# A streaming encoder layer on one core: earlier weights for the second unit, later gates in the last

## The chip, the cores and the metric

The kernel runs on one core of one Trainium2 chip. The metric is the time of one execution on the device in microseconds (us), the median of several runs. TensorE (PE in the profile) multiplies, VectorE (DVE), ScalarE (ACT) and GpSimd (POOL) do the elementwise work, and nearly all transfers are issued from the queue of SyncE (SP).

## The reference

One layer over 2048 prompt frames of one stream and 16 new frames of each of eight running streams (128 rows, with caches of 512 past positions). Rows are normed and modulated by a conditioning vector, then projected by `w_in` to ten groups of columns. A differential attention (four heads, two softmaxes each) and a stick-breaking attention (eight heads, a running product over the keys instead of a softmax) take three groups each; two groups are SiLU gates `za`, `zb`, and two are the merge gates `ga`, `gb`:

```python
qa, ka, va, za, qb, kb, vb, zb, ga, gb = jnp.split(h @ w_in, idx, axis=-1)
...
    ya = (oa.reshape(b, s, WIDTH_A) * jax.nn.silu(za)) @ w_branch_a
    yb = (ob.reshape(b, s, WIDTH_B) * jax.nn.silu(zb)) @ w_branch_b
    return (jax.nn.sigmoid(ga) * ya + jax.nn.sigmoid(gb) * yb) @ w_out
...
        xp = xp + gate * merge_branches(...)
...
    y_prompt = rms_norm(xp, final_g)
```

Everything is float32 outside. New keys and values are outputs too.

## The kernel before

Rows are worked in 17 tiles of 128: tiles 0 to 15 are the prompt, tile 16 (`NT`) is the sample. To keep float32 accuracy, each operand of a large product is split into a float16 high and low part, scaled by a power of two that comes from a norm of the matrix, and three products (high-high, high-low, low-high) are summed. So every weight block is loaded, squared and summed on ScalarE (`sum_squares`, L295), its scale is worked out (`scales`, on VectorE, with a product with ones on TensorE), and then it is split (`split`, L315 or L317 for the high part, L320 for the low).

The first stage norms and modulates the input and writes it transposed and split to `hT_d`. The middle stage, where most of the time goes, has eight units: unit u has head pair u // 2 and kind u % 2 (0 is the differential attention, 1 the stick-breaking). A step is a unit and a tile, 136 in all, the sample tile first in each unit. A step of a prompt tile makes the scores of its queries against all earlier keys (`scores`, products L697, L698, mask product L701), the softmax or the stick-breaking weights (for kind 1: sigmoids L131, scan L671, product on GpSimd L677, cast L605, rest L608), a transposing DMA (L615), and later the products with the values (L754 to L759). The weighted values go to `o_d`.

Beside attention, two lists of pieces are dealt out by hand:
- `line` holds the projections (24 products per tile, L461). In units of odd number each tile's projection is followed by 12 gate pieces of two products each (L537), which make 512 columns of the merge gates; ScalarE copies them out of the PSUM bank `ps_t` (L540) and they go to `g_d`. The line runs about `LEAD` = 5 steps ahead of attention. The input tile is fetched (`fetch_h`, L438) into one of three buffers `hs`, and is held there until its gate pieces have run.
- `side` pieces: `prepare_unit` loads, squares and splits the next unit's weights, in units with gates 22 pieces; `norms` has two lists, the squares of late weights and cached values (49 pieces, `spare`, loads L920) and the splitting of the cached keys (`cached`). `norm_at` and `keys_at` say in which steps they are dealt out.

When the line is empty, `early_work` prepares the output stage: the remaining branch weights and the first two tiles. The output stage (`branches` L1471, `output` L1508) runs over the tiles 0 to 14, then the sample tile, then tile 15, with the sample's attention as a second lane beside its first tiles. The conditioning gate of the sample tile has nine rows in `gate_d`, which are spread over its 128 rows by a product with `sel`.

The order of an engine's instructions is laid down when the kernel is built: a planner goes through the instructions in program order with a cost model and lets a later instruction pass one that is not yet ready. An instruction marked with `kept` passes no earlier one of its engine.

Of the kernel before, what the change touches and what calls it, by code (L numbers as in the profile page):

```python
# [17 lines left out]
F32 = mybir.dt.float32  # L18
# [3 lines left out]
AF = mybir.ActivationFunctionType  # L22
ALU = mybir.AluOpType
# [3 lines left out]
P = 128  # L27
# [31 lines left out]
H_AT = 2  # L59
Q_BUFS = 6  # L60
TR_AFTER = 5
LEAD = 5.0
TILE_TIME = 0.6
SAMPLE_TIME = 0.3
# [57 lines left out]
def layer_kernel(ctx: ExitStack, tc: tile.TileContext, a: dict):  # L122
# [14 lines left out]
    def kept(x):  # L137
        tc.keep_in_program_order(x)
        return x
# [68 lines left out]
    def bank(tag, dt=F32):  # L208
        return ps.tile([P, 512 if dt == F32 else 1024], dt, tag=tag, name=f"ps_{tag}", bufs=BANKS[tag])
# [222 lines left out]
    silu_z = {}  # L432
    at_hand, ahead, fetched = {}, {}, []

    def fetch_h(u, t):
        ahead[u, t] = hs[len(fetched) % 3].bitcast(F16).rearrange("p (f k n) -> p f k n", f=2, n=P)
        fetched.append(t)
        load(out=ahead[u, t], in_=hT_d[t // 4][:, t % 4, :, :, :])  # L438

    def project(U, t):  # L440
# [89 lines left out]
        def gate_piece(n):  # L530

            if n == 0:
                box["g"] = bank("t")
            for j in range(per * n, per * n + per):
                hi, wi = ((0, 0), (0, 1), (1, 0))[j % 3]
                k = j // 3
                T.matmul(box["g"][:, 0:gw], box["h"][:, hi, k, :], U["wg"][k // per][:, k % per, wi, :], start=(j == 0), stop=(j == 3 * KT - 1))  # L537
            if per * n + per == 3 * KT:
                gt = gts[:, 0:512]
                S.activation(out=gt[:, 0:gw], in_=box["g"][:, 0:gw], func=AF.Identity, scale=sc[:, 6:7])  # L540
                load(out=g_d[t][:, g0 : g0 + gw], in_=gt[:, 0:gw])

        return [lambda n=n: piece(n) for n in range(12)] + [lambda n=n: gate_piece(n) for n in range(3 * KT // per if gw else 0)]

    def transpose_qk(U, t):
        g, i = t // 4, t % 4
# [430 lines left out]
    def projection(m):  # L977
        u, t = steps[m]
        made = []

        def piece(i):
            if i == 0:
                begin(u, t)
                made.extend(project(units[u], t))
            if i == H_AT and not at_hand and m + 1 < len(steps) and steps[m + 1] not in ahead:
                fetch_h(*steps[m + 1])
            made[i]()

        return [lambda i=i: piece(i) for i in range(12 + 3 * GATES[u][1] // 128)]

    starts = []
    for m in range(len(steps)):
# [22 lines left out]
        return out  # L1015

    def norm_at(u, t):
        return u < 7 and t < NT and (t >= 7 if u == 0 else t >= 9 or u == 6)

    def keys_at(u, t):  # L1020
        return u in (1, 3, 5) and t < 8 or u in (2, 4, 6) and 9 <= t < 13
# [244 lines left out]
    branch_weights = list(range(8))  # L1266

    L = {}

    def cut(dst, st, src, k, j, s, n):  # L1270

# [118 lines left out]
    for n in range(len(steps) + 2):  # L1390
        made, qk, side = [], [], []
        if n < len(steps):
            u, t = steps[n]
            past += duration(t)
            if t == (3 if u == 0 else NT) and u < 7:
                back += prepare_unit(u + 1)
            if u == 7 and not back and not spare and not cached and len(branch_weights) > 1:
                side.append((1.0, branch_weight))
            for fn in back[: -(-len(back) // max(1, (W_READY if u else W_READY + 2) - t % NT))]:
                side.append((1.0, back.pop(0)))  # L1400
            for todo, here in ((spare, norm_at), (cached, keys_at)):
                if todo and here(u, t):
                    left = sum(here(*step) for step in steps[n:])
                    for _ in todo[: -(-len(todo) // left)]:
                        side.append((1.0, todo.pop(0)))
            if t < NT:
                qk = scores(units[u], t, made)
        target = position(len(steps) * past / whole + LEAD)
        pieces = take(target, min(n + 1, len(steps) - 1))
        if at[0] == len(line) and not pieces and not spare and not cached:  # L1410
            if cuts is None:
                cuts = early_work()
            pieces = [(1.0, fn) for fn in cuts[: -(-len(cuts) // (len(steps) + 2 - n))]]
            del cuts[: len(pieces)]
            if n == len(steps) + 1:
                while due and due[0][2] == 0.0:
                    due.pop(0)[3]()
                pieces += [(PV_B / PIECE, fn) for _, _, _, fn in due]
                due.clear()
        give(interleaved(pieces, qk, side), (PIECE, CHUNK, 0.0))  # L1420
# [5 lines left out]
    with ExitStack() as c2:  # L1426
# [28 lines left out]
            T.matmul(pg, sel[0:9, :] if i else ones[0:1, :], gsm[0:m, :], start=True, stop=True)  # L1455
            return pg

        def rows_of_gates():
            L["gsm"] = dec.tile([P, NB, P], F32, tag="dc", name="gsm", bufs=4).rearrange("p b n -> p (b n)")
            load(out=L["gsm"][0:9, :], in_=gate_d)  # L1460

        def branches(st):

            def half(j, br):
# [28 lines left out]
        def output(t, st, box):  # L1493

            def half(j):
                if j == 0:
                    box["x"] = s2.tile([P, D], F32, tag="x", name="x2", bufs=2)
                    load(out=box["x"], in_=x_rows(t))
                x = box["x"]
                c = slice(j * 512, (j + 1) * 512)  # L1500
                if t == NT:
                    pg = bank("ts"[j])
                    T.matmul(pg, sel[0:9, :], L["gsm"][0:9, c], start=True, stop=True)
                po = bank("o")
# [61 lines left out]
        for n in range(NT + 3):  # L1566
            work = branches(states[tiles[n]]) if n <= NT else []
            work += output(tiles[n - 1], states.pop(tiles[n - 1]), boxes[n - 1]) if 0 < n <= NT + 1 else []
            side = []
            if n + 2 <= NT:  # L1570
                states[tiles[n + 2]], stages = inputs(tiles[n + 2])
                side += [(IN_AT[i], stage) for i, stage in enumerate(stages)]
            if n + 1 <= NT:
                side += [(2, lambda n=n: turned(states[tiles[n + 1]], n + 1 >= MOVED)), (4.5, lambda n=n: opened(states[tiles[n + 1]]))]
            if n <= NT and tiles[n] == NT:
                side.append((3.3, rows_of_gates))
# [36 lines left out]
```

## Time and profile before

| | |
|---|---|
| runs (3) | 2240.26, 2244.19, 2244.84 us; median 2244.19 |
| profiled execution | 2238.37 us, its span 2236.6 us |
| mean granted clock of TensorE | 0.975 |
| busy share of PE, DVE, ACT, POOL | 93%, 78%, 72%, 31% |
| DMA traffic | 450.00 MB, 201 GB/s on average |

The middle stage begins at about 130 us and ends at about 1780 us. Times within the profiled execution are counted from the span's start. Busy time of PE is modelled and pipelined: a product of 512 columns has a duration of 0.379 us in the trace, while in a row of them the next starts earlier.

### The profile page before, as it was taken

How to read it: one execution, taken by the hardware profiler on the slowest of the kernel's cores; microseconds unless marked ns; L12 is line 12 of the kernel's file. 1: busy time of each engine (PE TensorE's matmuls, PEld its weight loads, DVE VectorE, ACT ScalarE, POOL GpSimd, SP SyncE). 2: the span in 40 equal slices, each digit the busy share in tenths (PEclk: the TensorE clock that was granted, in tenths of full speed). 3: DMA queues.
4: the chain of work that ended last, by engine and by line, in shares of the span. 5: the costliest groups of instructions: out<-in, count | busy, mean ns of one | idle time of the engine just before them, and what ended most of it. 6: DMA issues, size and time to landing. Idle time of an engine off the chain costs nothing. (4 is left out here: it accounts for less than half of the span.)

```text
span 2236.6 us, 41454 instructions
## 1 busy us (share of the span) xinstructions
PE 2068.9 (93%) x14608; PEld 1115.8 (50%) x14608; DVE 1747.9 (78%) x3799; ACT 1606.9 (72%) x3212; POOL 700.4 (31%) x608
## 2 busy tenths in 40 slices
PE   5998999999999999999999998999998689999997
PEld 3654555555555455555544554555554334444443
DVE  4657868889887788988778888787778868888864
ACT  3967877789887778987677788876577666676531
POOL 1122014446420343752024356301334512211210
PEclk8999999999999999999999999999999699999999
DMA  9777768889797989978879899675667899899762
GB/s 331 257 247 177 168 153 208 198 212 208 194 248 163 226 205 199 213 209 215 198 191 222 187 219 207 188 165 130 148 154 170 168 254 267 230 247 241 194 170 66
DMA packets 824672, 450.00 MB, mean 201 GB/s; under 512 B 556081, under 2 KB 763233, under 8 KB 823950
## 3 DMA queue, kind: packets, MB, share of 16 engines
q1 hardware_dynamic: 823514, 446.96, 80.9%
q8 instruction: 114, 1.87, 0.3%
q14 instruction: 96, 0.79, 0.1%
q10 hardware_dynamic: 948, 0.39, 0.1%
HBM read 228.82 MB, written 86.02 MB: 141 GB/s over the span
## 5 line engine op out<-in xcount | busy, mean ns | idle before, releaser
L677 POOL TENSOR_TENSOR sc_p<-sc_p,sc_n 128x127 f32<-128x127 f32 (+7 forms) x192 | 313.2, 1634 | 663.9 <-DVE sc_n L671 514.1
L461 PEld LDWEIGHTS <-hs 128*128 128x128 f16 x3120 | 292.2, 98 | 312.4 <-issue 4.3
L461 PE MATMUL ps_mm<-wa,hs 128*128 128x512 f16 x1590 | 383.8, 380 | 1.5 <-DVE v L320 0.9
L461 PE MATMUL ps_mm<-wb,hs 128*128 128x512 f16 x1530 | 379.7, 379 | 1.0 <-DVE qbuf L496 1.0
L537 PE MATMUL ps_t<-wb,hs 128*128 128x512 f16 x1224 | 291.8, 379 | 3.2 <-DVE qst L565 2.9
L671 DVE TENSOR_TENSOR_SCAN sc_n<-ps_s,sc_n,zero_t 128x512 f32<-128x512 f32 x192 | 245.4, 1278 | 36.0 <-ACT ps_s L131 30.7
L697 PE MATMUL ps_s<-k,qst 128*128 128x512 f16 (+3 forms) x640 | 224.2, 351 | 38.8 <-DVE sc_n L671 26.8
L608 DVE TENSOR_TENSOR sc_n<-sc_p,sc_n 128x128 f16<-128x128 f32 (+7 forms) x192 | 221.8, 1157 | 39.7 <-ACT sc_n L605 39.2
L537 PEld LDWEIGHTS <-hs 128*128 128x128 f16 x1632 | 154.7, 98 | 182.6 <-DVE qst L565 7.3
L131 ACT ACTIVATE sc_p<-ps_s,usc 128x512 f32<-128x512 f32 (+3 forms) x320 | 203.2, 635 | 36.2 <-PE ps_s L698 22.6
L698 PE MATMUL ps_s<-k,qst 128*128 128x512 f16 (+3 forms) x640 | 225.0, 352 | 0.0
L605 ACT CAST sc_n<-sc_p 128x128 f16<-128x128 f32 (+7 forms) x192 | 154.8, 807 | 63.8 <-POOL sc_p L677 63.0
L131 ACT ACTIVATE ps_s<-ps_s,usc 128x512 f32<-128x512 f32 (+3 forms) x320 | 195.5, 611 | 0.0
L758 PE MATMUL ps_o<-v,wt 128*128 128x128 f16 x1088 | 135.5, 226 | 22.5 <-DMA wt<-sc_n 22.5
L1508 PE MATMUL ps_o<-wo,wb 128*128 128x512 f16 x624 | 142.3, 384 | 0.8 <-ACT wb L1282 0.8
L591 DVE TENSOR_SCALAR_CACHE_REDUCE sc_p<-ps_s,usc 128x512 f32<-128x512 f32 (+3 forms) x160 | 106.1, 664 | 31.8 <-PE ps_s L698 17.5
L758 PEld LDWEIGHTS <-wt 128*128 128x128 f16 x1088 | 103.1, 102 | 51.3 <-DMA wt<-sc_n 28.5
L759 PE MATMUL ps_o<-v,wt 128*128 128x64 f16 x1088 | 127.8, 199 | 0.0
L1517 POOL TENSOR_TENSOR x<-m,x 128x512 f32<-128x512 f32 x32 | 48.1, 1504 | 251.2 <-DVE m L1512 164.5
L671 DVE TENSOR_TENSOR_SCAN sc_n<-ps_s,zero_t 128x128 f32<-128x128 f32 (+3 forms) x128 | 104.2, 814 | 23.8 <-ACT ps_s L131 23.0
L502 POOL TENSOR_TENSOR rot<-pr,rope 128x256 f32<-128x256 f32 x68 | 56.7, 833 | 205.5 <-ACT pr L475 109.9
L754 PE MATMUL ps_o<-v,wt 128*128 128x128 f16 x544 | 101.5, 224 | 19.2 <-DMA wt<-sc_n 19.0
(379 smaller groups left out, 4547.9 us busy)
## 6 DMA issues: line engine op xcount, KB each, us to landing
hs<-hT_d SPq DMA_DIRECT2D x130, 512.0 KB, 4.6
g_d<-gt SPq DMA_DIRECT2D x68, 256.0 KB, 3.3
out_dram<-pr SPq DMA_DIRECT2D x204, 64.0 KB, 3.6
wa<-in_w_in_dram SPq DMA_DIRECT2D x34, 256.0 KB, 5.7
o_d<-o SPq DMA_DIRECT2D x136, 64.0 KB, 2.2
wa<-g_d SPq DMA_DIRECT2D x17, 512.0 KB, 4.7
wb<-g_d SPq DMA_DIRECT2D x17, 512.0 KB, 4.9
hs<-o_d SPq DMA_DIRECT2D x17, 512.0 KB, 4.5
```

The lines of the kernel that those rows point to most:

```text
L131: i = S.activation(**kw)
L461: T.matmul(box["p"], box["h"][:, hi, k, :], U["w"][k][:, wi, :], start=(n == 0), stop=(n == 3 * KT - 1))
L537: T.matmul(box["g"][:, 0:gw], box["h"][:, hi, k, :], U["wg"][k // per][:, k % per, wi, :], start=(j == 0), stop=(j == 3 * KT - 1))
L605: x = S.copy(out=hi, in_=src)
L608: V.tensor_tensor(out=lo, in0=src, in1=hi, op=ALU.subtract)
L671: V.tensor_tensor_scan(out=dst[:, lo : lo + n][:, ::-1], data0=src[:, 0:n][:, ::-1], data1=zero_t[:, 0:1].to_broadcast([P, n]), initial=fi ...
L677: G.tensor_tensor(out=p[:, 0:m], in0=p[:, 0:m], in1=n[:, 1 : m + 1], op=ALU.mult)
L697: T.matmul(p[:, 0:n], qst[:, c, :], kk[:, c, 0:n], start=True, stop=False)
L698: T.matmul(p[:, 0:n], qst[:, 2 + c, :], kk[:, c, 0:n], start=False, stop=not diag)
L758: T.matmul(po[:, c * P : (c + 1) * P], wt[:, wj, :], vt[:, c, :, :], start=first, stop=False)
L759: T.matmul(po[:, c * P : c * P + 64], wt[:, nb + wj, :], vt[:, c, 0, :], start=False, stop=last)
L1508: T.matmul(po, st["y"][:, yi * 8 + k, :], wo[j * 4 + k // 2][:, wi, k % 2, :], start=(n == 0), stop=(n == 3 * KT - 1))
```

## The change

The preparation of unit 1's weights begins in unit 0's step of tile 1, not 3, and is spread so that it ends with tile 5, not 10. The late norms are no longer dealt out in unit 0 (`t >= 16` never holds there), so that the last of them come in unit 6. In unit 7 the gate pieces of tiles 11 to 15 leave the line; they are dealt out when it is empty, first those of tiles 13 to 15, whose input is still in `hs`, then those of 11 and 12, whose input is fetched again. The first product of each of these pieces and the copy out of PSUM are `kept`. `early_work` follows them. At the end, the rows of the sample's conditioning gate are no longer loaded once ahead; `gate_rows` loads half of them for each half of the sample tile, behind its products, into a buffer of the tag that `m` has too. The sample tile's row norm and store have a later place beside the last tile.

```diff
+LATE, LATE_DONE = 5, 1
...
+    def late(u, t):
+        return u == 7 and NT - LATE <= t < NT
...
-                T.matmul(box["g"][:, 0:gw], ...)
+                x = T.matmul(box["g"][:, 0:gw], ...)
+                if late(U["u"], t) and j == per * n:
+                    kept(x)
...
-                S.activation(out=gt[:, 0:gw], in_=box["g"][:, 0:gw], func=AF.Identity, scale=sc[:, 6:7])
+                x = S.activation(out=gt[:, 0:gw], in_=box["g"][:, 0:gw], func=AF.Identity, scale=sc[:, 6:7])
+                if late(U["u"], t):
+                    kept(x)
...
-        return [lambda n=n: piece(n) for n in range(12)] + [lambda n=n: gate_piece(n) for n in range(3 * KT // per if gw else 0)]
+        U["gates", t] = box, [lambda n=n: gate_piece(n) for n in range(3 * KT // per if gw else 0)]
+        return [lambda n=n: piece(n) for n in range(12)] + ([] if late(U["u"], t) else U.pop(("gates", t))[1])
...
+    def late_gates(t):
+
+        def piece(i):
+            box, made = units[7]["gates", t]
+            if i == 0:
+                if t < NT - 3:
+                    box["h"] = ahead[8, t]
+            made[i]()
+            if i == len(made) - 1 and t >= NT - 3 and NT - LATE + t - (NT - 3) < NT - 3:
+                fetch_h(8, NT - LATE + t - (NT - 3))
+
+        return [lambda i=i: piece(i) for i in range(3 * GATES[7][1] // 128)]
...
-        return u < 7 and t < NT and (t >= 7 if u == 0 else t >= 9 or u == 6)
+        return u < 7 and t < NT and (t >= 16 if u == 0 else t >= 9 or u == 6)
...
+    behind = [fn for t in list(range(NT - 3, NT)) + list(range(NT - LATE, NT - 3)) for fn in late_gates(t)]
...
-            if t == (3 if u == 0 else NT) and u < 7:
+            if t == (1 if u == 0 else NT) and u < 7:
                 back += prepare_unit(u + 1)
...
-            for fn in back[: -(-len(back) // max(1, (W_READY if u else W_READY + 2) - t % NT))]:
+            for fn in back[: -(-len(back) // max(1, (W_READY if u else 6) - t % NT))]:
                 side.append((1.0, back.pop(0)))
...
-            if cuts is None:
-                cuts = early_work()
-            pieces = [(1.0, fn) for fn in cuts[: -(-len(cuts) // (len(steps) + 2 - n))]]
-            del cuts[: len(pieces)]
+            todo = behind
+            left = max(1, len(steps) - LATE_DONE - n)
+            if not behind:
+                if cuts is None:
+                    cuts = early_work()
+                todo, left = cuts, len(steps) + 2 - n
+            pieces = [(1.0, fn) for fn in todo[: -(-len(todo) // left)]]
+            del todo[: len(pieces)]
...
-        def rows_of_gates():
-            L["gsm"] = dec.tile([P, NB, P], F32, tag="dc", name="gsm", bufs=4).rearrange("p b n -> p (b n)")
-            load(out=L["gsm"][0:9, :], in_=gate_d)
...
-                if t == NT:
-                    pg = bank("ts"[j])
-                    T.matmul(pg, sel[0:9, :], L["gsm"][0:9, c], start=True, stop=True)
...
-                    V.tensor_tensor(out=m, in0=m, in1=pg, op=ALU.mult)
+                    V.tensor_tensor(out=m, in0=m, in1=gate_rows(1, j), op=ALU.mult)
...
-            if n > NT:
-                side += [(0.6, lambda n=n: normed_rows(tiles[n - 2], boxes[n - 2])), (1.1, lambda n=n: stored_rows(tiles[n - 2], boxes[n - 2]))]
-            elif n > 1:
+            if n > 1:
                 side += [(1, lambda n=n: normed_rows(tiles[n - 2], boxes[n - 2])), (2.5, lambda n=n: stored_rows(tiles[n - 2], boxes[n - 2]))]
```

More of the change, by code (lines that the diff above doesn't have):

```diff
@@ L536, in gate_piece @@
                 k = j // 3
-                T.matmul(box["g"][:, 0:gw], box["h"][:, hi, k, :], U["wg"][k // per][:, k % per, wi, :], start=(j == 0), stop=(j == 3 * KT - 1))
+                x = T.matmul(box["g"][:, 0:gw], box["h"][:, hi, k, :], U["wg"][k // per][:, k % per, wi, :], start=(j == 0), stop=(j == 3 * KT - 1))
+                if late(U["u"], t) and j == per * n:
+                    kept(x)
             if per * n + per == 3 * KT:
                 gt = gts[:, 0:512]
-                S.activation(out=gt[:, 0:gw], in_=box["g"][:, 0:gw], func=AF.Identity, scale=sc[:, 6:7])
+                x = S.activation(out=gt[:, 0:gw], in_=box["g"][:, 0:gw], func=AF.Identity, scale=sc[:, 6:7])
+                if late(U["u"], t):
+                    kept(x)
                 load(out=g_d[t][:, g0 : g0 + gw], in_=gt[:, 0:gw])
-        return [lambda n=n: piece(n) for n in range(12)] + [lambda n=n: gate_piece(n) for n in range(3 * KT // per if gw else 0)]
+        U["gates", t] = box, [lambda n=n: gate_piece(n) for n in range(3 * KT // per if gw else 0)]
+        return [lambda n=n: piece(n) for n in range(12)] + ([] if late(U["u"], t) else U.pop(("gates", t))[1])
     def transpose_qk(U, t):
@@ L987, in piece @@
             made[i]()
-        return [lambda i=i: piece(i) for i in range(12 + 3 * GATES[u][1] // 128)]
+        return [lambda i=i: piece(i) for i in range(12 + (0 if late(u, t) else 3 * GATES[u][1] // 128))]
+    def late_gates(t):
[8 more added lines that the diff above has]
+        return [lambda i=i: piece(i) for i in range(3 * GATES[7][1] // 128)]
     starts = []
@@ L1574, in layer_kernel @@
                 side += [(2, lambda n=n: turned(states[tiles[n + 1]], n + 1 >= MOVED)), (4.5, lambda n=n: opened(states[tiles[n + 1]]))]
-            if n <= NT and tiles[n] == NT:
-                side.append((3.3, rows_of_gates))
-            if n > NT:
-                side += [(0.6, lambda n=n: normed_rows(tiles[n - 2], boxes[n - 2])), (1.1, lambda n=n: stored_rows(tiles[n - 2], boxes[n - 2]))]
-            elif n > 1:
+            if n > 1:
                 side += [(1, lambda n=n: normed_rows(tiles[n - 2], boxes[n - 2])), (2.5, lambda n=n: stored_rows(tiles[n - 2], boxes[n - 2]))]
```

## The prediction

> **What bounds the kernel now.** I read the page first, then the stretches table over the three places that the change touches, then the queues there.
>
> ```profile
> span 2236.6 us, 41454 instructions
> PE 2068.9 (93%) x14608; PEld 1115.8 (50%) x14608; DVE 1747.9 (78%) x3799; ACT 1606.9 (72%) x3212; POOL 700.4 (31%) x608
> ...
> PE   5998999999999999999999998999998689999997
> ...
> PEclk8999999999999999999999999999999699999999
> ```
>
> TensorE is busy 93% of the span, and nearly everywhere. An edit that leaves its work as it is can only win where TensorE waits. The slices (55.9 us each, counted from 0) show such places: slice 0, slice 3, slices 30 to 32, where the clock falls too, and the last. The change touches all but the first. The columns of the next view are start and end, length, busy PE, weight loads, DVE, ACT, POOL (each with its count), granted clock, DMA share, GB/s.
>
> ```profile
> 140.00:190.00 50.00, 49.56 (x286) 24.75 (x285) 34.24 (x110) 29.61 (x69) 14.82 (x19) 1.00 0.83 232
> 190.00:240.00 50.00, 36.54 (x268) 22.05 (x267) 41.29 (x125) 44.67 (x110) 9.97 (x12) 0.90 0.64 155
> ...
> 200.00:240.00 40.00, 26.54 (x193) 16.39 (x192) 32.95 (x101) 34.67 (x87) 7.79 (x9) 0.87 0.48 120
> 240.00:280.00 40.00, 39.34 (x295) 22.08 (x293) 32.23 (x82) 31.26 (x68) 0.00 (x0) 0.96 0.80 185
> 280.00:320.00 40.00, 40.00 (x278) 22.05 (x277) 25.60 (x65) 28.40 (x63) 2.26 (x4) 1.00 0.54 134
> ...
> 640.00:690.00 50.00, 45.48 (x333) 25.35 (x332) 40.21 (x108) 34.82 (x77) 2.24 (x2) 1.00 0.96 229
> ...
> 1660.00:1720.00 60.00, 59.66 (x428) 31.82 (x426) 46.43 (x68) 45.01 (x88) 21.49 (x16) 1.00 0.78 164
> 1720.00:1768.00 48.00, 26.71 (x221) 15.50 (x219) 45.98 (x52) 38.86 (x64) 29.69 (x16) 0.76 0.68 132
> ```
>
> From 200 to 240 us TensorE is idle for 13.46 of 40 us while ScalarE is near its limit (44.67 of 50 from 190 to 240). Before and after it TensorE is full and the others have room. From 1660 to 1720 it is full; from 1720 to 1768 VectorE is (45.98 of 48), and TensorE is busy 26.71.
>
> **Part 1: unit 1's weights earlier, no norms in unit 0.** Why does TensorE run dry at 200? The queue of SyncE and the first gate product of unit 1 tell:
>
> ```profile
> 155.38 1.04 ACT L295 ACTIVATE junk<-wa 128x1024 f16<-128x1024 f32 x1
> ...
> 163.27 1.04 ACT L295 ACTIVATE junk<-wa 128x1024 f16<-128x1024 f32 x1
> ...
> 192.40 0.46 SPq L438 DMA_DIRECT2D hs<-hT_d  x1
> 247.11 0.53 SPq L438 DMA_DIRECT2D hs<-hT_d  x1
> ...
> 239.64 4.45 PE L537 MATMUL ps_t<-wa,hs 128*128 128x512 f16 x12 [2.50 <-ACT qst L565]
> ...
> 221.42 1.30 DVE L320 SCALAR_TENSOR_TENSOR wb<-wb,sg,wb 128x1024 f16<-128x1024 f32 x1
> ```
>
> For 55 us no tile of the input is fetched. There are three such buffers (hs); each is held until its tile's gate product has run, and the last gate weight is split only at 221.42. So the line of projections stands, and attention runs alone on VectorE and ScalarE. With 22 preparation pieces in steps 1 to 5 instead of 3 to 10, the gate weights are ready some 40 us earlier: the steps whose squares of w now run at 155 to 164 us hold the splits of the gates too. What leaves ScalarE's full stretch:
>
> ```profile
> L295 ACT ACTIVATE junk<-wb 128x1024 f16<-128x1024 f32 x4 | 4.2, 1049 | 0.0
> L295 ACT ACTIVATE junk<-wa,g 128x1024 f16<-128x1024 f32 x3 | 3.4, 1142 | 0.0
> L315 ACT ACTIVATE wb<-wb,sg 128x1024 f16<-128x1024 f32 x2 | 2.3, 1140 | 0.0
> L315 ACT ACTIVATE wa<-wb,sg 128x1024 f16<-128x1024 f32 x1 | 1.1, 1140 | 0.0
> ```
>
> 4.2 + 3.4 + 2.3 + 1.1 = 11.0 us: the squares of the gates, the late norms and the splits. Gain: 13.46 us of idle TensorE, or, counting the 13% that the clock lacks over 40 us as well, 13.46 + 5.2 = 18.7 us at most. It won't all come back: unit 3 starts with its weights in time, and TensorE still idles 4.5 of 50 us there (640 to 690). So 13.46 - 4.5 = 9 up to 18.7 - 4.5 = 14; I take 12, near what ScalarE loses.
>
> The row 280 to 320 shows that 22.05 us of weight loads go with 40 full us; 16.39 then stand for 29.7, so that 10.3 are missing from 200 to 240. The Trainium skill, Perfetto Trace Analysis, section Identifying the Most-Contended Engine, says that matmul busy time misleads about TensorE's headroom and that weight-load busy time should be used; by that the gain would be 10.3 - 4.5 = 6 us and my total 6 us later. I keep the matmuls' idle time, because this stretch has more short products per load than the other.
>
> Where the pieces go, from 140 to 190, TensorE is full (49.56) and hides them: ScalarE has 29.61 + 4.2 + 3.4 = 37 of 50, VectorE 34.24 + 4 x 1.3 = 39. Without this cover they would cost up to 7.6 us on ScalarE. Their loads are issued earlier on the SyncE queue, behind which the rope and input loads stand; at a share of 0.83 I cost that at nothing, at most one piece of 0.5 us each.
>
> **The norms go to unit 6.** 49 pieces over one per step: now unit 0 has 9, units 1 to 5 have 35, unit 6 has 5. Afterwards units 1 to 5 have 35 and unit 6 has 14. Nine loads of 512 KB and nine squares with their readout move there:
>
> ```profile
> 1400.00:1440.00 40.00, 37.66 (x256) 20.16 (x255) 31.37 (x94) 35.05 (x82) 14.49 (x17) 1.00 0.68 197
> 1440.00:1480.00 40.00, 35.57 (x260) 20.11 (x259) 35.23 (x99) 29.66 (x75) 11.25 (x10) 1.00 0.66 178
> 1480.00:1520.00 40.00, 39.95 (x286) 22.18 (x285) 31.40 (x84) 27.61 (x59) 0.00 (x0) 1.00 0.69 141
> ...
> L295 ACT ACTIVATE junk<-wb x4: 1040/1052/1058, 1397.9 to 1413.4; 128x1024 f16<-128x1024 f32 x4
> L295 ACT ACTIVATION_READ_ACCUMULATOR junk<-wb x4: 186/189/201, 1398.8 to 1414.3; 128x1 f32 x4
> ```
>
> 9 x (1.05 + 0.19) = 11.2 us. ScalarE has 92.3 of 120 us there and would have 103.5 (86%). TensorE covers most; it idles 6.8 us in these rows. These squares keep their place in ScalarE's queue, so a late load holds what is behind them: the exponentials of attention. Bounds -1 (ScalarE is freer in units 0 and 1) and +11.2; I take +2.
>
> **Part 2: the last gates.** The stretch 1660 to 1720 has them:
>
> ```profile
> L537 PE MATMUL ps_t<-wb,hs x88: 379/379/389, 1658.7 to 1717.4; 128*128 128x512 f16 x88
> L537 PE MATMUL ps_t<-wa,hs x30: 379/379/379, 1659.6 to 1714.4; 128*128 128x512 f16 x30
> ...
> 2198.91 5.34 PE L1471 MATMUL ps_mm<-wb,wb 128*128 128x512 f16 x24
> ...
> PE ps_s L697 <- DVE sc_n L671: 13.2, 12, 2.7
> ...
> 1730.14 0.31 PE L701 MATMUL ps_s<-masks,idb 128*128 128x128 bf16 x1
> 1747.65 0.22 PE L701 MATMUL ps_s<-masks,idb 128*128 128x128 bf16 x1
> ```
>
> 118 of the 120 products of tiles 11 to 15 fall in it. Twenty-four products in a row take (5.34 - 0.38) / 23 = 0.216 us each (0.38 is one product's own length), so 120 take 25.9. Without them VectorE is the bound: at the 96% that it reaches after 1720, its 46.43 us need 48.5. This gives 60 - 48.5 = -11.5 us.
>
> Their new place is one step, that of tile 14 (the line is exhausted in the step of tile 13, and one step before the end all 60 pieces must be out). The masks' products show that step's length: 1730.14 to 1747.65, 17.5 us, bound by the scan (the wait row). TensorE's share of the tail's work in it is 26.71 x 17.5 / 48 = 9.7; with 25.9 that is 35.6, or 18 us too many, if the queue were in the order of the steps. That is the upper price. The lower is zero: over the whole tail, 26.71 + 25.9 = 52.6 stand against 48 us, 4.6 over, and the clock of 0.76 says that the 26.71 are partly slow time (at full clock 20.3, sum 46.2, which fits). The Trainium skill, TensorE: Matmul & The Clock Gate, section What's actually happening, says that the array runs at half rate after an idle window and at full rate after a busy one; by that the filled tail fits, and my price of +5.5 below would be about 0. Which is it? The gate pieces may not pass an earlier product, while later scores may pass a gate that waits; one bank (ps_t) serves all five tiles, so each waits for ScalarE's copy of the last, and scores slip in then. I take +5.5: net -6 for part 2, bounds -11.5 and +6.5. Five copies (L540, ScalarE) and the stores move too, and two input tiles are fetched again; the tail's DMA share of 0.68 takes these. Queued behind: the first tiles of the output stage need the same hs buffers, but its first products wait for w_out anyway.
>
> **Part 3: the end.** The gate rows of the sample tile:
>
> ```profile
> hs<-hT_d SPq DMA_DIRECT2D x130, 512.0 KB, 4.6
> g_d<-gt SPq DMA_DIRECT2D x68, 256.0 KB, 3.3
> ...
> 2174.74 0.72 SPq L1460 DMA_DIRECT2D gsm<-gate_d  x1
> 2224.85 1.06 ACT L295 ACTIVATE junk<-x 128x1024 f16<-128x1024 f32 x1
> 2226.03 0.15 DVE L274 TENSOR_SCALAR r<-facc 128x1 f32<-128x1 f32 x1 [2.07 <-ACT junk L295]
> 2229.32 1.28 DVE L1540 SCALAR_TENSOR_TENSOR x<-x,rF,gt 128x1024 f32<-128x1024 f32 x1
> ```
>
> The load issued at 2174.74, long before its use, becomes two loads issued when a buffer of m comes free; two broadcast products wait for them, with the last tile's products behind on TensorE. The nearest rows are the page's DMA issues, 3.3 and 4.6 us to landing, so +0 to +4 if one wait shows. The sample's row scale (L274) goes behind the last half's additions; L1540's 1.28 us stays ahead of the last tile's scaling either way: -0.5 to +1.5. I take +1 for both.
>
> **Sum.** The profiled execution took 2238.4 (span 2236.6 and 1.8 around it). -12 + 2 - 6 + 1 = -15: 2223.4. It lies 5.8 below the median of the runs, 2244.2; against that I forecast 2229.
>
> **Rivals.**
> - *The gates hold up attention (slower).* In queue order the 60 pieces stand before tile 15's scores, and VectorE starves: +18 in the tail. From the point where the steps before save less than 6 of their 11.5 (chains of scan, product on POOL and cast, not TensorE, setting their pace), part 2 costs 12 or more and, with +2 and +1, beats part 1's gain: about +3 to +8, 2250. For it: the step's sum of 35.6 against 17.5. Against: the one bank, and the scan's 13.2 us of holding up TensorE.
> - *Attention, not the missing weights, bounds 200 to 240.* Then part 1 gives 4 (the late norms' 3.4 and their readouts), and with a neutral part 2: -4 + 2 + 0 + 1 = -1, 2243. For it: ScalarE's 44.67 of 50. Against: the 55 us without a fetch.
> - *Both come in full:* -14 - 11.5 + 0 + 0 = -25.5, 2219; with -18.7, 2214.
> - *The order does nothing*, since the planner already moves work: the loads of unit 1's w were issued far ahead. Against: the gates' splits did run late.
>
> **Chances.** My forecast 0.53, full gain 0.20, no change (attention bounds 200 to 240, or the planner) 0.11, held attention 0.16. About 0.2% (4.5 us) is what a measurement of this kernel can tell from no change. Faster by more than that: 0.53 + 0.20 = 0.73, within: 0.11, slower: 0.16. The range reaches from the full gain, 2214, to 2247, into the slow case; most of that case and what lies beyond the bounds are left out.
>
> **What would show it.** Right: no gap in the fetches from 192 to 247, gate products from about 195, ScalarE below 42 of 50 from 190 to 240, TensorE full until 340; VectorE near 96% from tile 10's step on, with gate products among the scans of tiles 14 and 15, and the clock at 1.0 there. Wrong: a hole in VectorE while gate products run in a block; squares in unit 6 with idle ScalarE before them; a TensorE wait for gsm in the last 40 us.

## The result and the profile after

The changed kernel takes 2223.86 us (median of 6 runs, 2219.11 to 2227.34), the kernel before 2242.65 us on the same chip (2237.54 to 2244.84). The ratio is 0.9915, its 95% interval 0.9897 to 0.9932: 18.8 us or 0.85% less. The forecast was 2229, with a range of 2214 to 2247. The profiled execution took 2223.88 us; the sum in the prediction had put it at 2223.4.

The page of the changed kernel, its first lines and the slices of TensorE's work and clock:

```profile
span 2222.1 us, 41482 instructions
...
PE 2067.4 (93%) x14608; PEld 1115.0 (50%) x14608; DVE 1747.4 (79%) x3799; ACT 1606.1 (72%) x3212; POOL 703.0 (32%) x608
...
PE   5999999999999999999999998999998689999997
...
PEclk8999999999999999999999999999999799999999
```

The engines do the same work as before, to a few us. Slice 3 has filled from 8 to 9 tenths; the hole at slices 30 to 32 still has its 8, 6 and 8, though the clock of slice 31 is a tenth higher. The stretches, for unit 0's end, unit 1's start and the tail of attention (the columns are those of the prediction):

```profile
190.00:240.00 50.00, 43.68 (x325) 24.51 (x323) 42.60 (x124) 39.79 (x96) 9.89 (x11) 1.00 0.61 137
200.00:240.00 40.00, 33.68 (x268) 19.59 (x267) 33.96 (x100) 32.08 (x79) 5.90 (x8) 1.00 0.57 118
340.00:390.00 50.00, 48.34 (x324) 25.30 (x323) 45.33 (x75) 36.95 (x76) 22.29 (x21) 1.00 0.90 229
...
1640.00:1700.00 60.00, 53.21 (x408) 29.58 (x406) 56.01 (x87) 52.42 (x107) 26.08 (x20) 0.91 0.80 168
1700.00:1748.00 48.00, 41.85 (x310) 22.61 (x308) 37.03 (x41) 35.15 (x60) 24.14 (x14) 0.96 0.76 169
1712.00:1724.00 12.00, 11.32 (x101) 6.48 (x100) 9.29 (x12) 9.52 (x18) 4.85 (x3) 1.00 0.94 227
1724.00:1736.00 12.00, 10.76 (x83) 5.79 (x82) 8.32 (x10) 7.24 (x13) 7.13 (x5) 1.00 0.84 189
```

From 200 to 240 TensorE is busy for 33.68 us where it was 26.54: 7.1 of the 13.46 idle us are gone, and the clock is full. ScalarE is at 39.79 of 50 from 190 to 240, where it was at 44.67. In the tail VectorE is now the full engine before the last tiles (56.01 of 60), and then it is not (8.32 of 12 from 1724 to 1736) while TensorE runs the gates.

The line's fetches, the last split of the gate weights, and the first gate products of unit 1 (the gates are L541 here, the fetch L442):

```profile
176.98 2.47 DVE L321 SCALAR_TENSOR_TENSOR wa<-wb,sg,wa 128x1024 f16<-128x1024 f32 x2
204.26 0.38 SPq L442 DMA_DIRECT2D hs<-hT_d  x1
244.11 0.53 SPq L442 DMA_DIRECT2D hs<-hT_d  x1
...
L541 PE MATMUL ps_t<-wa,hs x120: 378/379/380, 232.0 to 298.8; 128*128 128x512 f16 x120
```

The gate weights are ready at 179.45 instead of 222.7, 43 us earlier, but the first gate product moves only from 239.6 to 232.0. The gap in the fetches is 40 us long instead of 55. So the place is right, and the step that was to explain it does not do so by itself.

### The profile page after: what moved, and what is told of

It reads as the page before. It is cut to its first block, busy times and chain, and to the rows that moved or that the text cites. A ratio compares the mean times of both kernels' runs of the same rounds, so it can differ in the third digit from the quotient of the medians.

```text
span 2222.1 us, 41482 instructions
## 1 busy us (share of the span) xinstructions
PE 2067.4 (93%) x14608; PEld 1115.0 (50%) x14608; DVE 1747.4 (79%) x3799; ACT 1606.1 (72%) x3212; POOL 703.0 (32%) x608
## 5 line engine op out<-in xcount | busy, mean ns | idle before, releaser
L465 PE MATMUL ps_mm<-wa,hs 128*128 128x512 f16 x1590 | 391.6, 382 | 5.2 <-DMA hs<-hT_d 5.2
L617 DVE TENSOR_TENSOR sc_n<-sc_p,sc_n 128x128 f16<-128x128 f32 (+7 forms) x192 | 213.5, 1114 | 43.4 <-ACT sc_n L614 42.8
L541 PEld LDWEIGHTS <-hs 128*128 128x128 f16 x1632 | 154.6, 98 | 178.6 <-DVE qst L574 5.0
L541 PE MATMUL ps_t<-wa,hs 128*128 128x512 f16 x1020 | 241.2, 379 | 2.0 <-DVE qst L574 2.0
L767 PE MATMUL ps_o<-v,wt 128*128 128x128 f16 x1088 | 137.2, 226 | 23.7 <-DMA wt<-sc_n 23.6
L541 PE MATMUL ps_t<-wb,hs 128*128 128x512 f16 x612 | 150.5, 380 | 3.9 <-DVE qst L574 1.7
L1494 PEld LDWEIGHTS <-wa 128*128 128x128 f16 x816 | 78.6, 99 | 93.2 <-issue 9.0
```

The source lines that it names most:

```text
L465: T.matmul(box["p"], box["h"][:, hi, k, :], U["w"][k][:, wi, :], start=(n == 0), stop=(n == 3 * KT - 1))
L541: x = T.matmul(box["g"][:, 0:gw], box["h"][:, hi, k, :], U["wg"][k // per][:, k % per, wi, :], start=(j == 0), stop=(j == 3 * KT - 1))
L617: V.tensor_tensor(out=lo, in0=src, in1=hi, op=ALU.subtract)
L767: T.matmul(po[:, c * P : (c + 1) * P], wt[:, wj, :], vt[:, c, :, :], start=first, stop=False)
L1494: T.matmul(pb, st["u"][:, ui * 8 + br * 4 + k, :], wb[br * 4 + k // 2 * 2 + j][:, wi, k % 2, :], start=(n == 0), stop=(n == 11))
```

## The experiments

Twelve kernels were run. The table gives each with the kernel before on its own chip; the ratio is the recorded one, which need not be the quotient of the two medians. The texts that follow were written before each run.

| kernel | median us | before us | ratio | 95% interval |
|---|---|---|---|---|
| prep | 2244.29 | 2243.27 | 0.9998 | 0.9985 to 1.0011 |
| norms | 2237.39 | 2243.27 | 0.997 | 0.9956 to 0.9984 |
| prep_norms | 2225.06 | 2243.27 | 0.9914 | 0.9898 to 0.993 |
| gates | 2238.86 | 2243.27 | 0.9975 | 0.9961 to 0.9989 |
| late_split | 2235.65 | 2242.18 | 0.9977 | 0.9966 to 0.9988 |
| old_end | 2221.96 | 2242.18 | 0.9915 | 0.9901 to 0.9928 |
| two_steps | 2219.99 | 2242.18 | 0.9896 | 0.988 to 0.9913 |
| not_kept | 2226.37 | 2242.18 | 0.9934 | 0.9916 to 0.9952 |
| prep_flush | 2228.66 | 2241.04 | 0.9941 | 0.9927 to 0.9955 |
| flush | 2228.72 | 2241.04 | 0.9949 | 0.9934 to 0.9963 |
| after_again | 2220.49 | 2244.04 | 0.9899 | 0.9875 to 0.9923 |
| two_old | 2221.34 | 2244.04 | 0.9893 | 0.9873 to 0.9913 |

**The parts by themselves.** *prep* is the kernel before with unit 1's weights early and nothing else:

```diff
-            if t == (3 if u == 0 else NT) and u < 7:
+            if t == (1 if u == 0 else NT) and u < 7:
...
-            for fn in back[: -(-len(back) // max(1, (W_READY if u else W_READY + 2) - t % NT))]:
+            for fn in back[: -(-len(back) // max(1, (W_READY if u else 6) - t % NT))]:
```

> Unit 1's weights early, norms as before. Theory 1 (late gate weights hold the input buffers, so TensorE runs dry): nearly the whole gain of units 0 and 1, -9 to -10 us. Theory 2 (ScalarE and VectorE bound attention from 190 to 240 us, and what counts is the work taken off ScalarE there): in proportion to the 7.6 of 11.0 us that leave it, -6 to -7.

*norms* is the kernel before with the late norms out of unit 0 alone:

```diff
-        return u < 7 and t < NT and (t >= 7 if u == 0 else t >= 9 or u == 6)
+        return u < 7 and t < NT and (t >= 16 if u == 0 else t >= 9 or u == 6)
```

> Only the norms leave unit 0, the weights as before. Theory 1: the line still stands until the gates are split, 0 to -1 there and +2 in unit 6: +1 to +2. Theory 2: 3.4 us of squares and their readouts leave ScalarE, -4 there and +2 in unit 6: -2.

*prep_norms* has both of these edits, which is the whole of part 1.

> Part 1 alone: unit 1's weights in steps 1 to 5 and no norms in unit 0, the last unit and the end as before. If the parts add up as the landmarks of the two traces say, about -9 to -10 us of unit 0 and 1 and +2 to +3 in unit 6: -7 us (ratio 0.997). If the change is all part 2, 0; if all part 1, -19.

*gates* is the changed kernel with these edits undone and with the end of the kernel before, which leaves part 2.

> Part 2 alone: the gates of the last five tiles behind all projections, units 0 to 6 and the end as before. Theory (59.66 of 60 us of TensorE relieved, then part of it given back where VectorE starves in the step of tile 14): -5 to -8 us. Rival (the moved gates hold up attention by as much as they free): 0 to +3.

The early weights bring nothing (ratio 0.9998), the norms 0.3%, both together 0.86%. So the parts of part 1 don't add; each hides what the other would gain. The last gates bring 0.25% by themselves, about 5.6 us by the ratio (the medians are 4.4 apart), near the prediction's -6. Neither theory stood for prep, and both sizes were wrong for norms and prep_norms: what the late norms cost in unit 0 had not been understood.

The gate products of unit 1 show how far ahead each kernel is at that unit's end. One row each, with the first and last start in us, for before (the row of the weight buffer that comes last), prep, norms, prep_norms and the changed kernel:

```profile
L537 PE MATMUL ps_t<-wb,hs x204: 379/379/380, 243.9 to 480.4; 128*128 128x512 f16 x102
```
```profile
L537 PE MATMUL ps_t<-wa,hs x408: 378/379/634, 243.2 to 479.7; 128*128 128x512 f16 x136
```
```profile
L537 PE MATMUL ps_t<-wa,hs x408: 379/379/631, 235.1 to 471.2; 128*128 128x512 f16 x136
```
```profile
L537 PE MATMUL ps_t<-wa,hs x408: 378/379/631, 229.7 to 466.8; 128*128 128x512 f16 x136
```
```profile
L541 PE MATMUL ps_t<-wa,hs x408: 378/379/389, 232.0 to 469.2; 128*128 128x512 f16 x136
```

480.4, then 479.7, 471.2, 466.8 and 469.2: prep is 0.7 us ahead of before, norms 9.2, prep_norms 13.6 and the changed kernel 11.2. Where each wins its lead is seen by following single products through the traces: the 601st product of TensorE, up to which all these kernels have the same order, and the first, 73rd, 265th and last of unit 1's 408 gate products (start in us; late_split and prep_flush come further down).

| kernel | 601st product | 1st gate | 73rd | 265th | last |
|---|---|---|---|---|---|
| before | 113.5 | 239.6 | 290.6 | 404.1 | 480.4 |
| prep | 114.6 | 243.2 | 287.4 | 403.4 | 479.7 |
| norms | 112.1 | 235.1 | 285.5 | 394.5 | 471.2 |
| prep_norms | 112.1 | 229.7 | 277.1 | 390.1 | 466.8 |
| late_split | 113.5 | 248.5 | 288.3 | 400.8 | 477.5 |
| prep_flush | 112.2 | 237.5 | 281.1 | 394.8 | 471.5 |
| changed | 113.2 | 232.0 | 278.7 | 392.5 | 469.2 |

At the 73rd gate product the changed kernel is 11.9 us ahead of before and prep_norms 13.5; up to the last neither gains more than 0.1. So their lead is won before 291 us, in the stretch that the change aims at. Prep has 3.2 us at that product and has lost 2.5 of them at the 265th. Norms has 5.1, and wins 4.5 more up to the 265th.

In that first stretch TensorE waits longest for the transposing DMA of the attention weights (`wt`), ahead of the products with the values. That wait from 185 to 260 us, in before, prep, norms and prep_norms:

```profile
PE ps_o L754 <- DMA wt<-sc_n: 7.7, 4, 5.0
```
```profile
PE ps_o L754 <- DMA wt<-sc_n: 7.5, 3, 3.7
```
```profile
PE ps_o L754 <- DMA wt<-sc_n: 3.9, 2, 3.5
```
```profile
PE ps_o L754 <- DMA wt<-sc_n: 2.9, 4, 1.2
```

It is 4.1 us in the changed kernel. With the weights early alone it stays. What makes these transfers late was not tried.

There is a second hole, which the prediction did not have. The stretch from 340 to 390, first in prep, then in norms:

```profile
340.00:390.00 50.00, 45.28 (x329) 25.02 (x330) 41.79 (x91) 35.19 (x76) 21.72 (x20) 1.00 0.87 216
```
```profile
340.00:390.00 50.00, 49.62 (x331) 26.21 (x332) 46.01 (x79) 38.01 (x80) 22.99 (x21) 1.00 0.98 225
```

TensorE is busy 45.28 of 50 us in prep (46.42 before) and 49.62 in norms. Among the waits from 300 to 410 are these, in before, prep, and the changed kernel (engine and line that waited, what it waited for, us in total, times, longest):

```profile
POOL wa L317 <- DMA keys_ak<-wa: 7.7, 5, 2.6
...
ACT junk L295 <- DMA wa<-in_cache_a_k_dram: 1.8, 1, 1.8
ACT wa L315 <- DMA keys_ak<-wa: 1.7, 3, 1.4
```
```profile
POOL wa L317 <- DMA keys_ak<-wa: 4.1, 3, 1.5
...
ACT wa L315 <- DMA keys_ak<-wa: 1.6, 3, 0.8
```
```profile
ACT junk L296 <- DMA wb<-in_cache_a_k_dram: 1.8, 1, 1.8
```

In steps 0 to 7 of unit 1 the cached keys are split in buffers of 4 KB per partition (`free`) that the weights and the late norms use too. Before, the splits wait for the store of an earlier result out of the same buffer; in the changed kernel and in norms none does. What the norms have to do with it is in the code: each norm piece squares what the piece before it loaded and then loads the next block. The ninth piece, the last in unit 0, loads a block that only the first piece in unit 1's step 9 squares. In the kernel before these are the ninth load, the next two, and the square:

```profile
L920 SPq DMA_DIRECT2D wb<-in_w_out_dram x1: 422/422/422, 262.9 to 262.9; - x1
...
L920 SPq DMA_DIRECT2D wb<-in_w_out_dram x2: 530/531/532, 404.7 to 419.0; - x2
...
414.81 1.10 ACT L295 ACTIVATE junk<-wb 128x1024 f16<-128x1024 f32 x1
```

One buffer of the pool is held for some 150 us, the whole time in which unit 1 splits its keys. That gave a new theory, that the norms hurt by this held buffer rather than by their squares. For the changed kernel the hole counts for little: from the 73rd to the 265th gate product it takes 113.8 us, the kernel before 113.5.

**The gate weights late again.** *late_split* is the changed kernel with the last four splits of unit 1's weights, those of the gates, held back to unit 0's step of tile 9:

```diff
-            for fn in back[: -(-len(back) // max(1, (W_READY if u else 6) - t % NT))]:
+            held = 4 if u == 0 and t < 9 else 0
+            for fn in back[: max(0, -(-(len(back) - held) // max(1, (W_READY if u else 6 if held else W_READY + 2) - t % NT)))]:
```

> The changed kernel, but the last four splits of the gate weights of unit 1 are held back until unit 0's step of tile 9; loads and squares stay early, no norms in unit 0. Theory 1 (the late gate weights hold the input buffers and so the line): the hole near 200 us comes back, 8 to 12 us slower than the changed kernel, 2232 to 2236. Theory 2 (what counts is that the late norms' 512 KB loads and their squares are gone from unit 0): 0 to 3 us slower, 2224 to 2227. PE's busy time from 190 to 240 would be about 37 of 50 by theory 1, 42 or more by theory 2.

It came out at 2235.65, in theory 1's range; of the gain 0.23% is left. TensorE's busy time from 190 to 240 fell from 43.68 to 40.14, nearer to theory 2's 42 than the 37 that were foreseen:

```profile
190.00:240.00 50.00, 40.14 (x284) 22.93 (x285) 44.07 (x123) 40.58 (x100) 13.76 (x14) 0.92 0.64 157
```

At the 73rd gate product late_split is 2.3 us ahead of before, where the changed kernel is 11.9. So early splits matter once the norms are gone. The test isn't pure: the blocks that wait for their split are in buffers of the same pool, which are held longer too. Whether the late weight or the longer hold costs the time, it can't tell.

**The held buffer by itself.** *prep_flush* is prep, with the nine norm pieces in unit 0 as before, except that the ninth squares and loads nothing. It has eight loads and eight squares in unit 0 and no buffer held:

```diff
+        more = iter(srcs)
...
-            if k < len(srcs):
-                src, dst, scale = srcs[k]
+            nxt = None if k in (8,) else next(more, None)
+            if nxt:
+                src, dst, scale = nxt
...
-        return [lambda k=k: one(k) for k in range(len(srcs) + 1)], ...
+        return [lambda k=k: one(k) for k in range(len(srcs) + 1 + len((8,)))], ...
```

> The kernel before with unit 1's weights early (as in prep) and the nine norm pieces still in unit 0, but the ninth squares what is loaded and loads nothing, so that no 4 KB buffer (wa or wb) is held by a half-done norm from the end of unit 0 to step 9 of unit 1. Theory A (that held buffer makes the splitting of the cached keys in unit 1 wait, and with it TensorE, from 340 to 400 us): 3 to 5 us faster than prep, 2239 to 2241, and the waits on the stores of the keys (keys_ak) are gone from 300 to 410 us. Theory B (the loads and squares of the norms in unit 0 cost by themselves): no change, 2243 to 2245.

2228.66 us, ratio 0.9941: one load less in unit 0 turns prep's 0.9998 into two thirds of the whole gain. That is more than theory A asked for, and theory B falls as the whole cause. None of the waits on keys_ak is left from 300 to 410; unit 1's last gate product starts at 471.5 against prep's 479.7, and TensorE is nearly full from 340 to 390:

```profile
L537 PE MATMUL ps_t<-wa,hs x408: 378/379/575, 237.5 to 471.5; 128*128 128x512 f16 x136
```
```profile
340.00:390.00 50.00, 48.80 (x323) 25.60 (x322) 45.53 (x78) 37.32 (x80) 22.40 (x21) 1.00 0.92 219
```

But the second hole is the smaller part of these 8.2 us. By the table above, prep_flush is 2.4 us ahead of prep at the 601st product, where the two kernels are still the same, and 6.3 at the 73rd gate product; only 1.9 come after it. TensorE's stretch from 190 to 240, in prep and in prep_flush:

```profile
190.00:240.00 50.00, 39.71 (x279) 22.43 (x276) 40.43 (x116) 38.22 (x95) 10.44 (x11) 0.93 0.72 172
```
```profile
190.00:240.00 50.00, 42.64 (x299) 24.34 (x296) 43.56 (x122) 40.21 (x97) 11.27 (x11) 0.90 0.66 166
```

Here TensorE's wait for `wt` (185 to 260) is 7.5 us in prep and 4.7 in prep_flush. All engines but SyncE have the same order in both up to about 335 us. SyncE's differs from about 198 us on, where prep_flush issues a load of cached keys ahead of weight loads that it follows in prep; the ninth load itself is issued only at 256.02 in prep. So the edit also moves transfers in the first stretch, a rival of theory A that was not tried by itself. The held buffer fits the waits and the hole from 340 to 390; that it makes the 0.57% between prep and prep_flush (12.8 us) is not shown.

The step from prep_flush to prep_norms (0.9941 to 0.9914), some 6 us, is what is left for the eight loads and squares themselves.

**The same buffer in units 3 and 5.** There a norm piece holds a buffer while the keys are split in both kernels. *flush* is the changed kernel with a piece that only squares at the end of units 2 and 4 (`k in (13, 27)` in the edit above).

> The changed kernel with two more norm pieces, at the end of units 2 and 4, that square and load nothing, so that no buffer is held while units 3 and 5 split their cached keys; two pieces more lie in unit 6. Theory A (the held buffer costs what it cost in unit 1): 4 to 8 us faster than the changed kernel, 2216 to 2220, and the waits on the stores of the keys are gone from 700 to 830 and from 1110 to 1240 us. Theory B: no change, 2223 to 2225.

2228.72 us, ratio 0.9949: slower than the changed kernel (0.9915 and, run once more, 0.9899). Yet what theory A says of the waits came true. The longest from 700 to 830 on a store of the keys, in the changed kernel, and the only one in flush:

```profile
POOL wa L318 <- DMA keys_ak<-wa: 9.7, 3, 4.2
```
```profile
POOL sc_p L686 <- DMA keys_ak<-wa: 1.6, 1, 1.6
```

And TensorE gains in that stretch. The changed kernel's rows, then those of flush:

```profile
720.00:780.00 60.00, 54.68 (x383) 29.78 (x381) 47.43 (x106) 41.07 (x93) 23.16 (x21) 1.00 0.89 221
790.00:850.00 60.00, 59.15 (x404) 30.97 (x402) 52.53 (x79) 47.75 (x99) 24.95 (x22) 1.00 0.93 204
```
```profile
720.00:780.00 60.00, 57.83 (x398) 31.44 (x397) 51.86 (x107) 44.92 (x100) 26.25 (x25) 1.00 0.97 239
790.00:850.00 60.00, 57.19 (x380) 29.34 (x379) 51.92 (x75) 43.82 (x92) 23.58 (x19) 1.00 0.86 182
```

3.2 us are won from 720 to 780, and 2.0 are lost again from 790 to 850. Unit 3's last gate product starts at 880.9 in flush and 880.0 in the changed kernel, unit 7's at 1740.3 and 1737.5, and the profiled execution is 8.8 us longer (2232.72): most of that comes behind attention, where neither of the two pieces lies. Why is open. The Trainium skill, Perfetto Trace Analysis, section Optimization Strategy, says that a gap which repeats on the full engine can mean too few buffers for the next tile. The waits that went away in units 1, 3 and 5 fit that. In unit 1 the kernel got shorter as well, for a cause that isn't settled; in units 3 and 5 it did not.

**The tail.** *old_end* is the changed kernel with `rows_of_gates` and the sample's late norm at their old places (the last parts of the diff of the change, undone).

> The changed kernel with the end of the kernel before: the nine gate rows loaded once ahead, the sample tile's row norm and store at the old places. The prediction priced the new end at +1 (-0.5 to +5.5), so this should come out 0 to 2 us faster, 2222 to 2224. Rival: the two loads are waited for and this gains 4 or more, 2220 or less. Second rival: the new order of the sample's row norm saves more than the loads cost, and this is slower by 1 or more.

*two_steps* deals the late gates over two steps:

```diff
-LATE, LATE_DONE = 5, 1
+LATE, LATE_DONE = 5, 0
```

> The changed kernel with the 60 late gate pieces dealt over the steps of tiles 14 and 15 instead of that of tile 14 alone. Theory 1 (the block of products in one step holds up the scores, which the hole of VectorE from 1688 to 1736 shows): 2 to 4 us faster, 2220 to 2222, VectorE over 11 of 12 from 1712 to 1736. Theory 2 (the end of attention is bound by VectorE's total work, and what follows starts later for each piece that comes later): 0 to 3 us slower, as the output stage's first pieces come behind the gates.

*not_kept* drops the marks on the late gates:

```diff
-                if late(U["u"], t) and j == per * n:
-                    kept(x)
...
-                if late(U["u"], t):
-                    kept(x)
```

> The changed kernel without the marks that forbid the late gates' first products and copies to pass earlier instructions: the planner may then move them ahead. Theory 1 (the planner then pulls the gates forward into steps 10 to 13, where TensorE is full, as in the kernel before): 3 to 6 us slower, 2227 to 2230. Theory 2 (the bank and the input fetched again set their place anyway): within 2 us of the changed kernel.

*after_again* is the changed kernel, and *two_old* has the edits of two_steps and old_end.

> The changed kernel itself once more, beside the next one on the same chip: 2220 to 2227. If what separates the profiles of kernels with the same order (up to 14 us at 1631 us) is drift of an execution and not the kernel, this profile lies several us from the first at the unit boundaries behind 600 us and within 1 us at 300 us.

> Both variants that came out faster: the late gates dealt over the steps of tiles 14 and 15, and the end of the kernel before. If their gains are real and add (about 4 and 2), 2217 to 2219, 4 to 6 us faster than the changed kernel beside it. Rival: both gains are within the spread of the runs, and this lies within 3 us of it, 2220 to 2223.

All of these lie between 2219.99 and 2226.37. Side by side, the changed kernel took 2220.49 and two_old 2221.34: the gains of two_steps and old_end, which looked like 4 and 2 us against 2223.86, are within the spread, as the rival for two_old had it. No kernel beat the changed one by more than its runs differ. two_steps did what it should at first, then not:

```profile
1700.00:1748.00 48.00, 40.79 (x312) 21.69 (x310) 41.61 (x43) 37.06 (x62) 27.74 (x15) 0.96 0.85 178
...
1724.00:1736.00 12.00, 9.38 (x67) 4.63 (x65) 8.22 (x9) 7.08 (x13) 6.41 (x4) 0.86 1.09 207
```

VectorE is busy 41.61 of 48 us instead of 37.03, but its hole from 1724 to 1736 stays (8.22 of 12) although half of the gates come later. not_kept is not told apart from the changed kernel either; in its profile the last gate product starts at 1743.1, in the changed kernel's at 1737.5, so the planner pulled nothing forward.

## Why the prediction was right, and where it was not

**The sum and the median.** The profiled execution was forecast at 2223.4 and took 2223.88. That it came so near is luck: six executions of the changed kernel took 2219.11 to 2227.34, and its terms were not that exact. The step that added 5.8 us to get from there to a median was wrong: the changed kernel's median is that of its profile, 2223.86. The kernel before was profiled in one of its short executions (2238.37, where its median is 2242.65). So the change is worth 18.8 us by medians, and 14.5 between the two profiled executions.

**Part 1, -12: right in place and size, for half of the reason.** The changed kernel is 11.9 us ahead at unit 1's 73rd gate product and 11.2 at its last, so the lead is won where it was forecast. By the ratio, part 1 with the norms moved gave 0.86%, 19 us (18.2 by medians), where -12 + 2 = -10 was forecast. A longer stretch gives a figure between the two. From TensorE's 601st product to the 581st product of L697, the first of each pair of score products (at 1618.7 in the kernel before), the two executions with the old order (before, gates) take 1505.2 and 1513.4 us, the seven with the new one (the changed kernel twice, prep_norms, old_end, two_steps, two_old, not_kept) 1490.4 to 1500.9: 13 us less on average.

The step that failed is that the late gate weights make the line stand and so TensorE run dry: with them 43 us earlier and the norms as before, prep had 3.2 us at the 73rd gate product, 0.7 at the last and nothing in the end. "No gap in the fetches from 192 to 247" and "gate products from about 195" did not come. The prediction showed the fetches and not what TensorE waited for; more than half of that was the transposing DMA (7.7 us), which early weights alone left at 7.5. What held the gates until 232 shows as no wait; they stand among attention's products in TensorE's queue, whose order the planner fixed, and that was not tried by itself. What was right: ScalarE below 42 of 50, the hole about half closed, and the clock at 1.00 there. The rival, by which the late weights don't bound this stretch and only the norms' removal counts, fits prep alone (0) but not the rest: norms gave 6.7 us by the ratio where -4 + 2 = -2 was expected, and with the norms gone the early weights are worth another 12 (0.997 to 0.9914). So neither of the two was the bound by itself. Why it takes both, and why prep_flush gets two thirds of the gain with one load less, stays open.

The two measures of TensorE's loss, the matmuls' idle time (gain 12) and the weight loads (gain 6; Perfetto Trace Analysis in the Trainium skill, section Identifying the Most-Contended Engine), are decided by the lead of 11.2 to 11.9 us: the idle time was the nearer here. Between 200 and 240 it fell by 7.1 us and the clock's share of 40 us by 5.2; the weight loads rose by 3.2.

**The norms in unit 6, +2.** Their squares there do not wait for loads, which the prediction had named as the sign of the upper bound. All instructions of that line from 1380 to 1500 in the changed kernel:

```profile
L296 ACT ACTIVATE junk<-wb x13: 1040/1063/1089, 1383.2 to 1493.6; 128x1024 f16<-128x1024 f32 x13
...
its engine sat idle before it (us, times) until:
```

No idle time stands before them. The +2 itself can't be told from drift in these profiles.

**Part 2, -6: right.** gates alone gave 0.9975, 5.6 us. On top of part 1 the ratios can't tell (0.9914 without part 2, 0.9915 and 0.9899 with parts 2 and 3). The traces can, when they are counted from that same product of L697, since up to it each of these kernels has the order of its partner without part 2. From there to the end, before takes 617.8 us and gates 611.7; prep_norms takes 620.2 and the changed kernel 610.8 and 611.2. So it is 6.1 us alone and about 9 on top of part 1, and 4 to 5 of them are there at the last product of L697. All five profiles without part 2 take 617.8 to 621.9 us from there, all nine with it 609.5 to 617.4. That prep_norms' profiled execution is nearly as short as those of the changed kernel (2224.57 against 2223.88 and 2220.11) comes from ahead of that product: it was there 8.8 and 4.6 us earlier, with the same order of instructions. For the runs without a profile it is not known.

The terms show, too. TensorE's clock is 1.00 from 1712 to 1736 with the gates in the hole, and VectorE stands for 2.7 and 3.7 of 12 us there, about the +5.5 that a step of 35.6 us in 17.5 was to cost. The Trainium skill, TensorE: Matmul & The Clock Gate, section What's actually happening, has the array at full rate after a busy window, from which the prediction worked out a cost of about 0: the clock rose as the page says, and VectorE stood all the same. "A hole in VectorE while gate products run in a block" was listed as a sign that the forecast was wrong, and it came; its size is that of the middle case, not the rival's 18.

**Part 3, +1: within the spread.** old_end is 1.9 below one median of the changed kernel and 1.5 above the other. TensorE does not stand for the loads; the nine-row products (L1482) have 0.7 us of idle time before them, and that is put down to no load:

```profile
L1482 PE MATMUL ps_t<-gsm,sel x4: 587/640/692, 2197.2 to 2206.3; 9*128 9x512 f32 x4
...
its engine sat idle before it (us, times) until:
  issue: 0.7, 2
```

From TensorE's 14461st product, up to which the two have the same order of products, to the end the changed kernel takes 42.3 us in both profiles and old_end 42.5.

## What to carry to other kernels

Two edits that aim at the same loss can be worth nothing and little alone, and much together, so try each alone and both. Before naming the cause of a hole, read what the full engine waits for in it. A gap that closes need not shorten the kernel: follow one and the same product through the traces, and see where the lead is won. Where two kernels have the same order up to some instruction, count from that instruction; the drift before it then falls out. Ask also what a piece of work holds while it waits for its next half: taking out one load at a unit's boundary moved waits and transfers well away from it.

## What had not been expected

Executions drift at places that have nothing to do with an edit. The changed kernel, after_again, prep_norms, two_steps, two_old, old_end and not_kept have the same order of instructions on every engine up to about 1580 us. Their last gate products of unit 1 start within 4.6 us (466.8 in prep_norms to 471.4 in not_kept), those of unit 5 within 9.5 us. Much of the 4.6 us is older than the middle stage: the 601st product starts at 111.8 to 116.0 us in these seven, and counted from there their last gate products of unit 1 lie within 1.5 us. The rows of unit 5 with the extremes, prep_norms and then not_kept:

```profile
L537 PE MATMUL ps_t<-wa,hs x306: 376/379/380, 1045.0 to 1288.9; 128*128 128x512 f16 x153
```
```profile
L541 PE MATMUL ps_t<-wa,hs x306: 376/379/380, 1055.4 to 1298.4; 128*128 128x512 f16 x153
```

So a plain difference of a few us between two profiles behind several hundred us says nothing of an edit, and medians of six runs of one program still differed by 3.4 us (2223.86 and 2220.49).
